# Issue order of the wide and narrow products in a split-precision decoder trunk

## The chip, the cores and the metric

The kernel runs on one core of a Trainium2 chip. The metric is the device time of one execution in microseconds (us). Three runs of the kernel before gave 2563.05, 2563.5 and 2563.72 us; the median is 2563.5 us.

## What is computed

A trunk of two pre-norm residual layers over 256 tokens of width 2048, in float32. Layer 0 mixes tokens with a Mamba-2 state-space mixer, layer 1 with a short gated convolution; each is followed by a gated feed-forward block with a convolution, and a norm closes the trunk.

```python
def reference(x, ...):
    for i in range(DEPTH):                       # DEPTH = 2
        h = rms_norm(x, mix_norm_w[i])
        if i % 2 == 0:
            x = x + ssd_mixer(h, ...)            # h @ (2048 x 10304), conv, scan, gate, @ (4096 x 2048)
        else:
            x = x + short_conv_mixer(h, ...)     # h @ (2048 x 6144), conv, gate, @ (2048 x 2048)
        h = rms_norm(x, ffn_norm_w[i])
        x = x + conv_ffn(h, ...)                 # h @ (2048 x 11264), conv, silu(g) * v, @ (5632 x 2048)
    return rms_norm(x, final_norm_w)
```

Nearly all of the arithmetic is the matrix products with the weights, some 115 M weights in all, each used once for 256 tokens.

## The kernel before

A weight matrix is streamed in units of 256 rows by 512 columns (`KU = 2` blocks of 128 rows, `COLS = 512`): one DMA brings a unit into `raw`, ScalarE rounds it to the matmul type (`wh`, L287), VectorE subtracts to get the rest (`wl`, L288). `wh` and `wl` have four buffers each (`WB = 4`), so a new unit is written when the unit four before it has been used up. The activations are held in the same two parts, side by side in one tile: `hl` has 256 columns of high part and then 256 of low part.

`stream` multiplies one block of 512 weight columns with all the rows. Its output is four column blocks `t` of 128, on the partitions of two PSUM tiles: `pts[0]` holds column blocks 0 and 1, `pts[1]` blocks 2 and 3; there are three such tiles in PSUM. For each unit it goes over `t` and, inside, over the two row blocks `k`; a (`t`, `k`) is one wide product (L334: `wh` against high and low part together, 512 columns) and one narrow product (L335: `wl` against the high part, 256 columns), added up in the same place of PSUM. Each has its own 128x128 stationary operand, so each comes with a weight load (PEld). With `one=True` (the streams for B, C and xs of the state-space mixer, where all must end in one 256-column sum) the wide product is made as two narrow ones (L331, L332). After the last unit `evac` reads both PSUM tiles out. There are 96 calls of `stream`; the down projection of the last layer has its own loop (L858 to L860, all products 512 wide).

The program is recorded in the order of the Python code, and a scheduler then puts the instructions of each engine in an order of its own choice, by when it reckons that operands are ready; only instructions given to `pin` keep the recorded order. The first stream of all (`before` given) is pinned. Small products of other kinds ("aux": transposes, sums over tokens, the scan of the mixer) are put in between.

Of the kernel before, what the change touches and what calls it, by code (L numbers as in the profile page):

```python
# [8 lines left out]
F32 = mybir.dt.float32  # L9
# [7 lines left out]
P = 128  # L17
T = 256
D = 2048
NKD = D // P  # L20
DI = 4096
NG = 8
# [3 lines left out]
DS = 128  # L26
# [6 lines left out]
KU = 2  # L33
COLS = 512
WB = 4
# [4 lines left out]
def trunk_kernel(ctx, tc, a, out):  # L40
    nc = tc.nc
    mm = nc.tensor.matmul
# [13 lines left out]
    psm = ctx.enter_context(tc.tile_pool(name="psm", bufs=3, space=PSUM))  # L56
    psa = ctx.enter_context(tc.tile_pool(name="psa", bufs=2, space=PSUM))

    n_id = [0]

    def uid(s):
        n_id[0] += 1
        return f"{s}_{n_id[0]}"
# [11 lines left out]
    start = ExitStack()  # L75
    tokpool = start.enter_context(tc.tile_pool(name="tokpool", bufs=1))
    xt = tokpool.tile([P, 2, D], F32, tag="xt", name="xt")
    pin = tc.keep_in_program_order
# [44 lines left out]
    base, at = {}, 0  # L123
    pieces = [[] for _ in range(nrt)]
    for name, r in rows:
        base[name] = at
        lo = 0
        while lo < r.shape[0]:
            i, off = divmod(at, P)
            n = min(P - off, r.shape[0] - lo)  # L130
# [3 lines left out]
        if name == "mix":  # L134
            n_mix, at = at, P
# [90 lines left out]
    plan = []  # L226
# [31 lines left out]
    raws, units = [], []  # L258
    taken = [0]

    def load_raw():
        i = len(raws)
        w, c0, kc = plan[i]
        raw = rawpool.tile([P, KU, COLS], F32, tag="raw", name=uid("raw"))
        for k in range(0, KU, 1 if i == 0 else KU):
            n = 1 if i == 0 else KU
            ins = nc.sync.dma_start(
                out=raw[:, k : k + n, :],
                in_=w[(kc + k) * P : (kc + k + n) * P, c0 : c0 + COLS].rearrange(
                    "(k p) n -> p k n", p=P  # L270
                ),
            )
            if i < NKD // KU + 2:
                pin(ins)
        raws.append(raw)

    def load_unit():
        i = len(units)
        if i == len(raws):
            load_raw()  # L280
        raw, raws[i] = raws[i], None
        wh = wpool.tile([P, KU, COLS], F32R, tag="wh", name=uid("wh"))
        wl = wpool.tile([P, KU, COLS], F32R, tag="wl", name=uid("wl"))
        units.append((wh, wl))

        def half(ks, put):
            put(nc.scalar.copy(wh[:, ks, :], raw[:, ks, :]))  # L287
            put(tt(  # L288
                out=wl[:, ks, :], in0=raw[:, ks, :], in1=wh[:, ks, :].bitcast(F32),
                op=ALU.subtract,  # L290
            ))

        if i == 0:
            return half
        with tc.high_priority(0 if i < NKD // KU else None):
            half(slice(0, KU), pin if i < NKD // KU + 2 else lambda ins: ins)

    def weight_unit(c0, kc, ahead=WB - 1):

        i = taken[0]  # L300
        assert plan[i][1:] == (c0, kc), (plan[i], c0, kc)
        taken[0] += 1
        while len(units) < min(i + ahead + 1, len(plan)):
            load_unit()
        got, units[i] = units[i], None
        return got

    def stream(c0, hls, kcs, evac, one=False, before=None):

        pts = [psm.tile([P, 2, 512], F32, tag="main", name=uid("main")) for _ in range(2)]
        n = len(kcs)
        put = (lambda ins: ins) if before is None else pin
        for u in range(0, n, KU):
            order = [(t, k) for t in range(4) for k in range(KU)]
            if before is not None and u == 0:
                before(0)
                order.sort(key=lambda tk: tk[1])  # L320
            wh, wl = weight_unit(c0, kcs[u], WB - 1 if before is None else 0)
            for at, (t, k) in enumerate(order):
                if before is not None and at == (0 if u else 2) and u + KU < n:
                    before(u // KU + 1)
                i = u + k
                o = pts[t // 2][:, t % 2, :]
                hl = hls[i // 2][:, i % 2, :]
                lw = slice(t * P, (t + 1) * P)
                first, last = i == 0, i == n - 1
                if one:  # L330
                    put(mm(o[:, 0:T], wh[:, k, lw], hl[:, 0:T], start=first, stop=False))  # L331
                    put(mm(o[:, 0:T], wh[:, k, lw], hl[:, T : 2 * T], start=False, stop=False))  # L332
                else:
                    put(mm(o, wh[:, k, lw], hl, start=first, stop=False))  # L334
                put(mm(o[:, 0:T], wl[:, k, lw], hl[:, 0:T], start=False, stop=last))  # L335
        if before is not None:
            before(n // KU)
        if taken[0] < len(plan):
            while len(units) < min(taken[0] + WB - 1, len(plan)):
                load_unit()  # L340
        for p in range(2):
            evac(p, pts[p])

# [7 lines left out]
    def scaled(pt, r, one=False, tag="tp", pool=None):  # L351
        if one:
            s = pair_tmp(tag, pool)
            tt(out=s, in0=pt[:, :, 0:T], in1=rep2(r), op=ALU.mult)  # L354
            return s
        s = pair_sum(pt)
        tt(out=s, in0=s, in1=rep2(r), op=ALU.mult)  # L357
        return s

    def conv(s, width, wname, nk, k0, bname=None, tag="tp", pool=None):  # L360

        y = pair_tmp(tag, pool)
        for j in range(2):
            w = pcol(wname, (width - 1) * nk + k0 + j)
            if bname is None:
                act(y[:, j, :], s[:, j, :], AF.Copy, scale=w)
            else:
                act(y[:, j, :], s[:, j, :], AF.Identity, bias=pcol(bname, k0 + j), scale=w)  # L368
            for d in range(1, width):
                stt(  # L370
                    out=y[:, j, d:T], in0=s[:, j, 0 : T - d],
                    scalar=pcol(wname, (width - 1 - d) * nk + k0 + j),
                    in1=y[:, j, d:T], op0=ALU.mult, op1=ALU.add,
                )
        return y
# [27 lines left out]
    xp, xhl = [], []  # L403
    ss = small.tile([P, 2, 4], F32, tag="ss", name="ss")
    first = {}
# [50 lines left out]
    def bc_stream(g, o, before=None):  # L456

        res = []

        def evac(p, pt):  # L460
            k0 = DI // P + o * NG + g + 2 * p
            s = scaled(pt, first["r0"], True)
            y = conv(s, W_SSD, "ssdw", NCX, k0, "ssdb", "bc", bcpool)
            act(y, y, AF.Silu)
            res.append(y)

        stream(2 * DI + o * NG * DS + g * DS, xhl, range(NKD), evac, True, before)
        return res

    load_raw()  # L470
# [293 lines left out]
    xhl, nhl = nhl, []  # L764
    r = norm.row()
    norm = Norm()
    for part in range(2):
        hid = ffn_part(0, part, xhl, r)
        last = part == 1
# [6 lines left out]
    xhl, nhl = nhl, []  # L776
# [32 lines left out]
    xhl = nhl  # L809
# [3 lines left out]
    for c in range(2):  # L813
        for q in range(4):
            ps = aux()
            for j in range(4):
                k = 4 * q + j
# [22 lines left out]
    for part in range(2):  # L840
        lo, hi = FPARTS[part]
        hid = ffn_part(1, part, xhl, r)
        n = hi - lo
        for cg in range(D // COLS):
            cols = slice(cg * COLS, (cg + 1) * COLS)
            pt = psm.tile([P, 2, 512], F32, tag="main", name=uid("main"))
            end = part == 1 and cg == D // COLS - 1
            lag = WB - 2 if end else 0
            held = {}

            def products(c, u):
                wh, wl = held[u]
                for k in range(KU):
                    i = u + k
                    hl = hid[i // 2][:, i % 2, :]
                    hi_ = hl[:, c * P : (c + 1) * P]
                    lo_ = hl[:, T + c * P : T + (c + 1) * P]
                    mm(pt[:, c, :], hi_, wh[:, k, :], start=(i == 0), stop=False)  # L858
                    mm(pt[:, c, :], hi_, wl[:, k, :], start=False, stop=False)  # L859
                    mm(pt[:, c, :], lo_, wh[:, k, :], start=False, stop=(i == n - 1))  # L860

            def evac(c):
                x = xtok[c][:, cols]
                tt(out=x, in0=pt[:, c, :], in1=x, op=ALU.add)  # L864
                if part == 1:
                    junk = tmp.tile([P, 512], F32, tag="tp", name=uid("tp"))
                    act(junk, x, AF.Square, accum_out=ss[:, c, cg : cg + 1])
                    tt(out=x, in0=x, in1=fin[:, cols], op=ALU.mult)
                if end:
                    finish(c)  # L870

            for u in range(0, n + lag * KU, KU):
                if u < n:
                    held[u] = weight_unit(cg * COLS, lo + u, 1 if end else WB - 1)
                    products(0, u)
                    if u == n - KU and end:
                        evac(0)
                if u >= lag * KU:
                    products(1, u - lag * KU)
            if not end:  # L880
                evac(0)
            evac(1)
# [30 lines left out]
```

## Time and profile before

| | us |
|---|---|
| median of three runs | 2563.5 |
| the profiled execution | 2563.32 |
| its span, first to last instruction | 2561.5 |
| TensorE matmul (PE) busy | 2544.6 |
| weight loads (PEld) busy | 2235.2 |
| VectorE (DVE) busy | 1790.2 |
| ScalarE (ACT) busy | 1321.5 |

A matmul's row lasts from its start until its result is out, and the next one starts well before that, so the mean length of a row says nothing of the rate. The rate is read from the starts: so many starts in a row, divided into the time from the first to the last. The timeline view gives starts to 0.01 us and merges neighbours of the same line into one row with a count (x2).

### The profile page before, as it was taken

The numbers are of one execution on the slowest core, as the hardware profiler recorded it, in microseconds if no ns is written. First come the engines' busy times: TensorE is split into PE (matmuls) and PEld (weight loads), VectorE is DVE, ScalarE is ACT, GpSimd is POOL, SyncE is SP. The second block draws the span as 40 slices with busy tenths as digits, with TensorE's granted clock in tenths as the row PEclk, the third lists the DMA queues.
The fourth block names the chain that finished last, engine by engine and source line by source line (L and its number), as shares of the span: only waits on it lengthen the run. The fifth ranks groups of instructions, "written<-read, shape, count | busy, mean of one in ns | idle before, by whom it ended". The sixth has DMA issues, their size and how long they took to land.

```text
span 2561.5 us, 38324 instructions
## 1 busy us (share of the span) xinstructions
PE 2544.6 (99%) x15101; PEld 2235.2 (87%) x15101; DVE 1790.2 (70%) x2601; ACT 1321.5 (52%) x1630; POOL 1.1 (0%) x8
## 2 busy tenths in 40 slices
PE   9999999999999999999999999999999999999998
PEld 9999998998888888888888888888888888888886
DVE  7888876788677776557776666666677774577765
ACT  5565643566555554345554444444555553455543
POOL 0000000000000000000000000000000000000000
PEclk9999999999999999999999999999999999999999
DMA  7666655665666665666665666666566666666664
GB/s 229 175 184 193 182 176 188 189 182 172 198 183 191 190 188 181 193 188 183 193 190 181 193 186 185 185 197 189 174 183 187 189 197 190 193 186 188 189 192 145
DMA packets 255737, 478.76 MB, mean 187 GB/s; under 512 B 17668, under 2 KB 29124, under 8 KB 255428
## 3 DMA queue, kind: packets, MB, share of 16 engines
q1 hardware_dynamic: 254643, 474.13, 61.3%
q8 instruction: 118, 1.93, 0.3%
q10 hardware_dynamic: 912, 2.18, 0.2%
q14 instruction: 64, 0.52, 0.1%
HBM read 474.09 MB, written 2.16 MB: 186 GB/s over the span
## 4 chain that ended last, share of the span: by engine, by line
PE 98%; DVE 1%; ACT 1%; DMA 0%; issue 0%; SPq 0%; DVEq 0%; ACTq 0%
PE main L334 50%; PE main L335 29%; PE main L331 3%; PE main L332 3%; PE main L858 3%; PE main L859 3%; PE main L860 3%; PE aux L649 1%; DVE wl L288 0%; PE aux L657 0%; DMA bias_bc<-in_ssd_dt_bias_dram 0%; PE aux L513 0%; PE aux L630 0%; DMA raw<-in_ssd_w_in_dram 0%; ACT wh L287 0%; PE aux L187 0%
## 5 line engine op out<-in xcount | busy, mean ns | idle before, releaser
L334 PE MATMUL main<-hl,wh 128*128 128x512 f32 x5568 | 1944.9, 396 | 0.2 <-DVE hl L218 0.2
L335 PE MATMUL main<-hl,wl 128*128 128x256 f32 x6336 | 1749.2, 281 | 1.8 <-DVE wl L288 1.8
L288 DVE TENSOR_TENSOR wl<-raw,wh 128x1024 fp32r<-128x1024 f32 (+1 forms) x881 | 1072.6, 1221 | 702.2 <-ACT wh L287 701.6
L287 ACT CAST wh<-raw 128x1024 fp32r<-128x1024 f32 (+1 forms) x881 | 920.8, 1048 | 1067.7 <-PE main L334 735.2
L334 PEld LDWEIGHTS main<-hl,wh 128*128 128x128 f32 x5568 | 1034.8, 188 | 236.7 <-issue 2.0
L335 PEld LDWEIGHTS main<-hl,wl 128*128 128x128 f32 x6336 | 1196.9, 189 | 17.6 <-DVE wl L288 2.7
L331 PE MATMUL main<-hl,wh 128*128 128x256 f32 x768 | 219.5, 287 | 2.5 <-DVE tp L354 1.3
L332 PE MATMUL main<-hl,wh 128*128 128x256 f32 x768 | 218.6, 285 | 0.0
L331 PEld LDWEIGHTS main<-hl,wh 128*128 128x128 f32 x768 | 148.2, 193 | 4.0 <-issue 2.0
L332 PEld LDWEIGHTS main<-hl,wh 128*128 128x128 f32 x768 | 148.3, 193 | 1.5 <-issue 1.1
L858 PE MATMUL main<-wh,hl 128*128 128x512 f32 x352 | 137.5, 391 | 0.8 <-DVE xtok L864 0.8
L859 PE MATMUL main<-wl,hl 128*128 128x512 f32 x352 | 137.4, 390 | 0.0
L860 PE MATMUL main<-wh,hl 128*128 128x512 f32 x352 | 137.0, 389 | 0.0
L370 DVE SCALAR_TENSOR_TENSOR tp<-tp,prm,tp 128x255 f32<-128x255 f32 x208 | 90.6, 477 | 0.0
L346 ACT COPY tp<-main 128x512 f32<-128x512 f32 x128 | 74.3, 580 | 26.0 <-PE main L335 26.0
L348 DVE TENSOR_TENSOR tp<-main,tp 128x512 f32<-128x512 f32 x128 | 87.4, 683 | 0.0
L858 PEld LDWEIGHTS main<-wh,hl 128*128 128x128 f32 x352 | 66.1, 188 | 15.3 <-DVE xtok L864 1.2
L860 PEld LDWEIGHTS main<-wh,hl 128*128 128x128 f32 x352 | 66.1, 188 | 14.2
L859 PEld LDWEIGHTS main<-wl,hl 128*128 128x128 f32 x352 | 66.1, 188 | 13.6
L370 DVE SCALAR_TENSOR_TENSOR g<-tp,prm,g 128x254 f32<-128x254 f32 (+1 forms) x176 | 74.6, 477 | 0.1
L368 ACT ACTIVATE g<-tp,prm,prm 128x256 f32<-128x256 f32 x88 | 48.2, 596 | 38.0 <-DVE tp L357 38.0
L357 DVE TENSOR_TENSOR tp<-tp,rrow 128x512 f32<-128x512 f32 x96 | 66.0, 688 | 1.8
(134 smaller groups left out, 966.9 us busy)
## 6 DMA issues: line engine op xcount, KB each, us to landing
raw<-in_ffn_w_up_dram SPq DMA_DIRECT2D x352, 512.0 KB, 3.7
raw<-in_ffn_w_down_dram SPq DMA_DIRECT2D x176, 512.0 KB, 4.1
raw<-in_ssd_w_in_dram SPq DMA_DIRECT2D x159, 512.0 KB, 4.5
raw<-in_sc_w_in_dram SPq DMA_DIRECT2D x96, 512.0 KB, 4.1
raw<-in_ssd_w_out_dram SPq DMA_DIRECT2D x64, 512.0 KB, 4.2
raw<-in_sc_w_out_dram SPq DMA_DIRECT2D x32, 512.0 KB, 4.2
cbc<-cs_d SPq DMA_DIRECT2D x32, 256.0 KB, 5.1
xt<-in_x_dram SPq DMA_DIRECT2D x8, 256.0 KB, 7.4
```

The lines of the kernel that those rows point to most:

```text
L287: put(nc.scalar.copy(wh[:, ks, :], raw[:, ks, :]))
L288: put(tt(out=wl[:, ks, :], in0=raw[:, ks, :], in1=wh[:, ks, :].bitcast(F32), op=ALU.subtract,))
L331: put(mm(o[:, 0:T], wh[:, k, lw], hl[:, 0:T], start=first, stop=False))
L332: put(mm(o[:, 0:T], wh[:, k, lw], hl[:, T : 2 * T], start=False, stop=False))
L334: put(mm(o, wh[:, k, lw], hl, start=first, stop=False))
L335: put(mm(o[:, 0:T], wl[:, k, lw], hl[:, 0:T], start=False, stop=last))
L346: nc.scalar.copy(pb, pt[:, :, T : 2 * T])
L348: tt(out=s, in0=pt[:, :, 0:T], in1=pb, op=ALU.add)
L370: stt(out=y[:, j, d:T], in0=s[:, j, 0 : T - d], scalar=pcol(wname, (width - 1 - d) * nk + k0 + j), in1=y[:, j, d:T], op0=ALU.mult, op1=ALU ...
L858: mm(pt[:, c, :], hi_, wh[:, k, :], start=(i == 0), stop=False)
L859: mm(pt[:, c, :], hi_, wl[:, k, :], start=False, stop=False)
L860: mm(pt[:, c, :], lo_, wh[:, k, :], start=False, stop=(i == n - 1))
```

## The change

Each (`t`, `k`) no longer goes wide, narrow. For each column block, `stream` now issues the wide products of both row blocks of a unit, and then both narrow ones. A new helper `follow` ties each of these products to the one before it, so that the scheduler keeps the recorded order; the loop of the last down projection is tied in the same way. The unit is worked in two halves: `pts[0]` with unit `u`, then `pts[1]` with unit `u - 1`; a unit is thus held over two steps, and `pts[1]` ends one half later. Weights are asked for two units ahead before the first half and three units ahead after the second. In the `one=True` streams the order in a column block is high, low, high, low, rest, rest. The first stream is now a function of its own, `first_stream`, with the order that it had.

```diff
+    def follow(inst):
+        if last_main[0] is not None:
+            tc.add_manual_dep(
+                inst.ins, last_main[0],
+                mybir.DependencyInfo(
+                    mybir.DependencyClass.NoSync, mybir.DependencyReason.DATA
+                ),
+                reason="stream order",
+            )
+        last_main[0] = inst.ins.name
+        return inst
...
+    def load_ahead(n):
+        while len(units) < min(taken[0] + n, len(plan)):
+            load_unit()
...
-    def stream(c0, hls, kcs, evac, one=False, before=None):
...
-        for u in range(0, n, KU):
-            order = [(t, k) for t in range(4) for k in range(KU)]
...
-                    put(mm(o, wh[:, k, lw], hl, start=first, stop=False))
-                put(mm(o[:, 0:T], wl[:, k, lw], hl[:, 0:T], start=False, stop=last))
...
+    def stream(c0, hls, kcs, evac, one=False):
+        pts = [psm.tile([P, 2, 512], F32, tag="main", name=uid("main")) for _ in range(2)]
+        n = len(kcs)
+        held = {}
+        def half(p, u):
+            wh, wl = held[u]
+            for t in (2 * p, 2 * p + 1):
+                o = pts[p][:, t % 2, :]
+                lw = slice(t * P, (t + 1) * P)
+                part = [(u + k, k, hls[(u + k) // 2][:, (u + k) % 2, :]) for k in range(KU)]
+                for i, k, hl in part:
+                    if one:
+                        for c in (0, T):
+                            follow(mm(
+                                o[:, 0:T], wh[:, k, lw], hl[:, c : c + T],
+                                start=(i == 0 and c == 0), stop=False,
+                            ))
+                    else:
+                        follow(mm(o, wh[:, k, lw], hl, start=(i == 0), stop=False))
+                for i, k, hl in part:
+                    follow(mm(
+                        o[:, 0:T], wl[:, k, lw], hl[:, 0:T], start=False, stop=(i == n - 1)
+                    ))
+        for u in range(0, n + KU, KU):
+            if u < n:
+                held[u] = weight_unit(c0, kcs[u], WB - 2)
+                half(0, u)
+            if u:
+                half(1, u - KU)
+            load_ahead(WB - 1)
         for p in range(2):
             evac(p, pts[p])
...
-                    mm(pt[:, c, :], hi_, wh[:, k, :], start=(i == 0), stop=False)
+                    follow(mm(pt[:, c, :], hi_, wh[:, k, :], start=(i == 0), stop=False))
```

PE's own order at the start of a stream of layer 0's first down projection, before: `main_10551` and `main_10552` are the PSUM tiles of the first and the second pair of column blocks, `wh`/`wl` with one number and the next are one unit's weights (10483, 10505, 10527 and 10555 are the first four units), `hl` a pair of row blocks of the activations.

```order
L334 MATMUL main_10551<-hl_8606,wh_10527 128x512
L335 MATMUL main_10551<-hl_8606,wl_10528 128x256
L334 MATMUL main_10551<-hl_8606,wh_10527 128x512
L335 MATMUL main_10551<-hl_8606,wl_10528 128x256
L334 MATMUL main_10551<-hl_8622,wh_10555 128x512
L334 MATMUL main_10552<-hl_8192,wh_10483 128x512
L335 MATMUL main_10552<-hl_8192,wl_10484 128x256
L334 MATMUL main_10552<-hl_8192,wh_10483 128x512
L335 MATMUL main_10552<-hl_8192,wl_10484 128x256
```

The same start of the stream on PE now (units 10491, 10513, 10535):

```order
L376 MATMUL main_10282<-hl_10278,wl_10470 128x256 x2
L374 MATMUL main_10551<-hl_8192,wh_10491 128x512 x2
L376 MATMUL main_10551<-hl_8192,wl_10492 128x256 x2
L374 MATMUL main_10551<-hl_8192,wh_10491 128x512 x2
L376 MATMUL main_10551<-hl_8192,wl_10492 128x256 x2
L374 MATMUL main_10551<-hl_8208,wh_10513 128x512 x2
L376 MATMUL main_10551<-hl_8208,wl_10514 128x256 x2
L374 MATMUL main_10551<-hl_8208,wh_10513 128x512 x2
L376 MATMUL main_10551<-hl_8208,wl_10514 128x256 x2
L374 MATMUL main_10552<-hl_8192,wh_10491 128x512 x2
```

Wide and narrow alternated, and the first pair of column blocks ran three units ahead of the second at a stream's start; now two wide go before two narrow, and the first pair is never more than two units ahead.

VectorE's order around the same place, before (`x_190` and `x_221` are the residual tiles that read out the two PSUM tiles of the stream that ended):

```order
L288 TENSOR_TENSOR wl_10506<-raw_10503,wh_10505 128x1024 [waits DMAHW6_49,PE_49,Activation_49]
L288 TENSOR_TENSOR wl_10528<-raw_10525,wh_10527 128x1024 [waits DMAHW7_49,PE_49,Activation_49]
L698 TENSOR_TENSOR x_190<-main_10281,x_190 128x512 [waits PE_49]
L698 TENSOR_TENSOR x_221<-main_10282,x_221 128x512 [waits PE_49]
L700 TENSOR_TENSOR x_190<-main_10281,x_190 128x512 [waits DVE_49]
L700 TENSOR_TENSOR x_221<-main_10282,x_221 128x512 [waits DVE_49]
L288 TENSOR_TENSOR wl_10556<-raw_10553,wh_10555 128x1024 [waits DMAHW0_49,Activation_49]
```

And now:

```order
L302 TENSOR_TENSOR wl_10514<-raw_10511,wh_10513 128x1024 [waits DMAHW6_49,PE_49,Activation_49]
L748 TENSOR_TENSOR x_190<-main_10281,x_190 128x512 [waits PE_49]
L750 TENSOR_TENSOR x_190<-main_10281,x_190 128x512 [waits DVE_49]
L302 TENSOR_TENSOR wl_10536<-raw_10533,wh_10535 128x1024 [waits DMAHW7_49,PE_49,Activation_49]
L748 TENSOR_TENSOR x_221<-main_10282,x_221 128x512 [waits PE_49]
L302 TENSOR_TENSOR wl_10564<-raw_10561,wh_10563 128x1024 [waits DMAHW0_49,Activation_49]
L750 TENSOR_TENSOR x_221<-main_10282,x_221 128x512 [waits DVE_49]
```

The four reads of PSUM stood together between two units; now a unit's subtraction stands between the first tile's reads and the second's.

## Rows read from the trace of the kernel before

**Rows 1.** The page: span, and busy us (share) xinstructions of each engine; clock granted per slice.
```profile
span 2561.5 us, 38324 instructions
PE 2544.6 (99%) x15101; PEld 2235.2 (87%) x15101; DVE 1790.2 (70%) x2601; ACT 1321.5 (52%) x1630; POOL 1.1 (0%) x8
...
PEclk9999999999999999999999999999999999999999
```
**Rows 2.** The page: the chain that ended last, its shares by engine and by line.
```profile
PE 98%; DVE 1%; ACT 1%; DMA 0%; issue 0%; SPq 0%; DVEq 0%; ACTq 0%
PE main L334 50%; PE main L335 29%; PE main L331 3%; PE main L332 3%; PE main L858 3%; PE main L859 3%; PE main L860 3%; PE aux L649 1%; DVE wl L288 0%; PE aux L657 0%; DMA bias_bc<-in_ssd_dt_bias_dram 0%; PE aux L513 0%; PE aux L630 0%; DMA raw<-in_ssd_w_in_dram 0%; ACT wh L287 0%; PE aux L187 0%
```
**Rows 3.** The page's groups: line, operation, count, busy us, mean ns, idle before.
```profile
L334 PE MATMUL main<-hl,wh 128*128 128x512 f32 x5568 | 1944.9, 396 | 0.2 <-DVE hl L218 0.2
L335 PE MATMUL main<-hl,wl 128*128 128x256 f32 x6336 | 1749.2, 281 | 1.8 <-DVE wl L288 1.8
L288 DVE TENSOR_TENSOR wl<-raw,wh 128x1024 fp32r<-128x1024 f32 (+1 forms) x881 | 1072.6, 1221 | 702.2 <-ACT wh L287 701.6
L287 ACT CAST wh<-raw 128x1024 fp32r<-128x1024 f32 (+1 forms) x881 | 920.8, 1048 | 1067.7 <-PE main L334 735.2
...
L331 PE MATMUL main<-hl,wh 128*128 128x256 f32 x768 | 219.5, 287 | 2.5 <-DVE tp L354 1.3
...
L858 PE MATMUL main<-wh,hl 128*128 128x512 f32 x352 | 137.5, 391 | 0.8 <-DVE xtok L864 0.8
```
**Rows 4.** Groups on PE, from 740 to 1140 us (layer 0's feed-forward block).
```profile
L334 PE MATMUL main<-hl,wh 128*128 128x512 f32 x1142 | 398.2, 396 | 0.0
```
**Rows 5.** Timeline of PE (start us, us), wide products alone, last layer's down projection.
```profile
2109.68 0.39 PE L858 MATMUL main<-wh,hl 128*128 128x512 f32 x1
...
2113.99 0.39 PE L859 MATMUL main<-wl,hl 128*128 128x512 f32 x1
```
**Rows 6.** Timeline of PE, narrow products alone, a `one=True` stream.
```profile
299.74 0.28 PE L335 MATMUL main<-hl,wl 128*128 128x256 f32 x1
...
302.50 0.28 PE L332 MATMUL main<-hl,wh 128*128 128x256 f32 x1
```
**Rows 7.** Timeline of PE, 1295 to 1303 us, feed-forward block.
```profile
1295.24 0.40 PE L334 MATMUL main<-hl,wh 128*128 128x512 f32 x1
...
1299.75 0.62 PE L334 MATMUL main<-hl,wh 128*128 128x512 f32 x2
1300.20 0.28 PE L335 MATMUL main<-hl,wl 128*128 128x256 f32 x1
1300.32 0.40 PE L334 MATMUL main<-hl,wh 128*128 128x512 f32 x1
...
1302.44 0.40 PE L334 MATMUL main<-hl,wh 128*128 128x512 f32 x1
1302.68 0.40 PE L335 MATMUL main<-hl,wl 128*128 128x256 f32 x2
1302.91 0.40 PE L334 MATMUL main<-hl,wh 128*128 128x512 f32 x1
```
**Rows 8.** Timeline of PE, 995 to 998 us, feed-forward block.
```profile
995.87 0.64 PE L334 MATMUL main<-hl,wh 128*128 128x512 f32 x2
996.35 0.28 PE L335 MATMUL main<-hl,wl 128*128 128x256 f32 x1
...
997.39 0.40 PE L335 MATMUL main<-hl,wl 128*128 128x256 f32 x2
997.63 0.40 PE L334 MATMUL main<-hl,wh 128*128 128x512 f32 x1
```
**Rows 9.** Waits: engine and line, waited for: us in total, times, longest us.
```profile
ACT wh L287 <- PE main L334: 735.2, 492, 6.1
...
PE main L335 <- DVE wl L288: 1.8, 3, 1.4
```
**Rows 10.** Busy us (x) of each engine from 100 to 250 us (state-space mixer).
```profile
100.00:250.00 150.00, 149.41 (x1084) 135.83 (x1083) 132.08 (x281) 96.26 (x116) 0.00 (x0) 1.00 0.66 191
```

More of the change, by code (lines that the diff above doesn't have):

```diff
@@ L59, in trunk_kernel @@
     n_id = [0]
+    last_main = [None]
+    def follow(inst):
[9 more added lines that the diff above has]
+        return inst
     def uid(s):
@@ L302, in weight_unit, with first_stream @@
         taken[0] += 1
-        while len(units) < min(i + ahead + 1, len(plan)):
-            load_unit()
+        load_ahead(ahead)
         got, units[i] = units[i], None
         return got
-    def stream(c0, hls, kcs, evac, one=False, before=None):
+    def first_stream(c0, hls, kcs, evac, before):
         pts = [psm.tile([P, 2, 512], F32, tag="main", name=uid("main")) for _ in range(2)]
         n = len(kcs)
-        put = (lambda ins: ins) if before is None else pin
         for u in range(0, n, KU):
@@ L317, in stream @@
             order = [(t, k) for t in range(4) for k in range(KU)]
-            if before is not None and u == 0:
+            if u == 0:
                 before(0)
                 order.sort(key=lambda tk: tk[1])
-            wh, wl = weight_unit(c0, kcs[u], WB - 1 if before is None else 0)
+            wh, wl = weight_unit(c0, kcs[u], 0)
             for at, (t, k) in enumerate(order):
-                if before is not None and at == (0 if u else 2) and u + KU < n:
+                if at == (0 if u else 2) and u + KU < n:
@@ L324, in stream @@
                     before(u // KU + 1)
                 i = u + k
-                o = pts[t // 2][:, t % 2, :]
+                o = pts[t // 2][:, t % 2, 0:T]
                 hl = hls[i // 2][:, i % 2, :]
                 lw = slice(t * P, (t + 1) * P)
[L329 to L333, printed above, removed]
-                    put(mm(o, wh[:, k, lw], hl, start=first, stop=False))
@@ L335, in stream @@
-                put(mm(o[:, 0:T], wl[:, k, lw], hl[:, 0:T], start=False, stop=last))
[L336 to L340, printed above, removed]
+                pin(mm(o, wh[:, k, lw], hl[:, 0:T], start=(i == 0), stop=False))
+                pin(mm(o, wh[:, k, lw], hl[:, T : 2 * T], start=False, stop=False))
+                follow(pin(mm(o, wl[:, k, lw], hl[:, 0:T], start=False, stop=(i == n - 1))))
@@ new lines, in first_stream @@
+        before(n // KU)
+        load_ahead(WB - 1)
+        for p in range(2):
+            evac(p, pts[p])
+    def stream(c0, hls, kcs, evac, one=False):
[27 more added lines that the diff above has]
+                half(1, u - KU)
+            load_ahead(WB - 1)
@@ L465, in evac @@
             res.append(y)
-        stream(2 * DI + o * NG * DS + g * DS, xhl, range(NKD), evac, True, before)
+        c0 = 2 * DI + o * NG * DS + g * DS
+        if before is not None:
+            first_stream(c0, xhl, range(NKD), evac, before)
+        else:
+            stream(c0, xhl, range(NKD), evac, True)
         return res
@@ L857, in products @@
                     lo_ = hl[:, T + c * P : T + (c + 1) * P]
-                    mm(pt[:, c, :], hi_, wh[:, k, :], start=(i == 0), stop=False)
-                    mm(pt[:, c, :], hi_, wl[:, k, :], start=False, stop=False)
-                    mm(pt[:, c, :], lo_, wh[:, k, :], start=False, stop=(i == n - 1))
+                    follow(mm(pt[:, c, :], hi_, wh[:, k, :], start=(i == 0), stop=False))
+                    follow(mm(pt[:, c, :], hi_, wl[:, k, :], start=False, stop=False))
+                    follow(mm(pt[:, c, :], lo_, wh[:, k, :], start=False, stop=(i == n - 1)))
             def evac(c):
```

## The prediction

> **What bounds the kernel now.** I read the page's first two parts, then the chain, then the groups, then the starts of products in the timeline. PE is busy 2544.6 of 2561.5 us at the full granted clock in every slice [rows 1], which is the level of 2.4 GHz. The chain that ended last runs over PE for 98% of the span, half of it in L334 and 29% in L335 [rows 2]; DVE and ACT have a part of 1% each. PE hardly waits for anybody: 1.8 us in all for the subtraction that makes `wl` [rows 3, 9]. So a change that does not make PE wait is worth what it changes in the rate at which PE takes one product after the other, and nothing else.
>
> That rate is read from starts. 400 us of the feed-forward block hold 1142 rows of L334 and nothing but wide and narrow products [rows 4]; 400/1142 is 350.3 ns for one wide and one narrow, and 350.6 if the one that had begun before the window is taken off. I use 350.5 ns for a pair. Products of one width alone run like this: wide, 19 starts in 4.31 us [rows 5], 226.8 ns each; narrow, 23 starts in 2.76 us [rows 6], 120.0 ns each. A wide and a narrow at these rates make 346.8 ns. So the alternation costs 3.7 ns a pair over what the two kinds take among their own.
>
> Where the 3.7 ns sit is seen in [rows 7]. From 1295.24 to 1299.75 there are 13 pairs in 4.51 us: 346.9 ns, nothing lost. Then two wide stand together (the scheduler had put them so), and from 1300.32 to 1302.44 there are 6 pairs in 2.12 us: 353.3 ns. The alternating stream thus has two rates, it keeps one for as long as the pattern is undisturbed, and a break in the pattern moves it to the other. The mean of 350.5 says that it spends a little over half of its time, (350.5 - 346.9)/(353.3 - 346.9) = 56%, at the slower one.
>
> **The change part by part.** The instructions are the same, in number and in shape: 5568 wide products, as many narrow ones among them (6336 less the 768 of the `one=True` streams) [rows 3], with the same weight loads. What changes is who stands beside whom.
>
> *The order in a column block.* The rows that come nearest to two wide, two narrow are the places where the scheduler left doubles. Two wide from their start to the next narrow one took 1300.20 - 1299.75 = 0.45 us in the fast stretch [rows 7], and 996.35 - 995.87 = 0.48 us in a slow one [rows 8]. Two narrow took 1302.91 - 1302.68 = 0.23 us [rows 7] and 997.63 - 997.39 = 0.24 us [rows 8]. So four products of the new order lie between 0.45 + 0.23 = 0.68 us and 0.48 + 0.24 = 0.72 us; four of the old one take 2 x 350.5 = 701 ns. By rows 5 and 6 they take 2 x 226.8 + 2 x 120.0 = 693.6 ns, and I take this value. The reason is in the same rows: a double of narrow ones took 0.23 to 0.24 us, its own rate or less, in both stretches, so that the wide pair behind it starts without a debt, and the wide pair that so starts is the one of 0.45 us; the 0.48 us stand only behind alternating products at the slow rate, which the new order does not have. It also halves the number of changes of width. The gain is 350.5 - 346.8 = 3.7 ns for each of 5568 pairs, 20.6 us. I do not count on all of it: streams end, small products come in between, and after each such break the order must find its rate again. I leave a tenth of the stretch at the slower rate of rows 7, 0.1 x (353.3 - 346.8) x 5568 = 3.6 us.
>
> *The `one=True` streams and the last down projection.* All products of the first have 256 columns, all of the second 512, so their order changes no neighbour's width: 120.0 and 226.8 ns before and after [rows 5, 6]. Nothing.
>
> *The second pair a unit behind.* A half unit is four pairs, 4 x 350.5 = 1.4 us. Before, a unit was read for two halves on end; now from its first use over three halves (its first, the next unit's first, its own second), so its buffer comes free 1.4 us later. There are four buffers and a unit lasts 2.8 us, so from free to needed again there were 8.4 us and are 7.0. In these the rounding on ACT (1.05 us) and the subtraction on DVE (1.22 us) must be done [rows 3], and what else stands in their queues. Queued behind a subtraction that waits on DVE are the reads of PSUM and the convolutions of the stream that ended, and behind those in turn the next units; on ACT the copies out of PSUM stand behind the rounding. At a stream's start the new order is the gentler one: before, the first pair of column blocks took three units and began a fourth in 4.2 us, now it takes two and then alternates with the second pair. The cover is seen in the waits: the rounding waited 492 times for PE to set a buffer free, up to 6.1 us, and PE 3 times for a subtraction [rows 9]. Losing 1.4 us of such a lead costs nothing where DVE has time. The least it has is in the mixer, 132 of 150 us busy [rows 10]; there I allow 0 to 3 us, and take 0.
>
> *The tie between products.* It adds no wait across engines. What the scheduler could pull forward when an operand was late it cannot now; it was late 3 times for 1.8 us [rows 9]. I bound this at 0 to 2 us and take 0. The DMA queue on SP sees the same loads in the same order.
>
> **The sum.** Against the profiled execution, 2563.3 us (its span and 1.8 us around it; the median of the three runs is 0.2 us higher): 2563.3 - 20.6 + 3.6 = 2546.3 us, 0.7% faster. I predict 2546 us.
>
> **The rivals.** A measurement of this kernel can tell 0.2% from no change, 5.1 us: below 2558.2 is faster, above 2568.4 slower.
>
> *A tax for each change of width.* The loss of 3.7 ns may hang on going from wide to narrow and back, wherever it happens, and be paid once for every four products now: half of it stays. 2563.3 - 10.3 = 2553 us. For it speaks that the streams of one width lose nothing [rows 5, 6]; against it that half the alternating stretches lose nothing either [rows 7].
>
> *The order does not matter.* The two doubles of wide products average 0.465 us and the two of narrow ones 0.235 us, 0.70 us together, which is two pairs as they are now [rows 4, 7, 8]. Then the new order also has two rates, spends as much time at each as the old one, and the time stays at 2563 us, within 2 us. [...]
>
> *A slower rate of its own.* The new order may lock, as the old one does, but at the doubles of rows 8: 0.48 + 0.24 = 0.72 us for four products, 19 ns over now, and since it is fixed nothing would ever move it off. That is 2784 x 19 ns = 53 us, 2616 us, if it held everywhere; it decides where the mean four reaches 701 + 1.8 ns (5.1 us over 2784 fours), that is where (702.8 - 693.6)/(720 - 693.6), a third of the fours, are of that kind. For it: such doubles exist. Against it: the narrow double after it in rows 8 was followed by the fast rate.
>
> *PE waits for weights.* The 1.4 us less of lead may be lacking at the ends of streams, where DVE and ACT also read PSUM out. It decides from (20.6 + 5.1)/96 = 0.27 us in each of the 96 streams; a subtraction's length, 1.22 us, in each would be 117 us less the gain, 2660 us. Against it stand rows 9 and the gentler start.
>
> **How the numbers follow.** The forecast, 2540 to 2549 us: 0.52. A tax for each change, 2549 to 2558: 0.16. The order does not matter, 2558 to 2568: 0.15. A slower rate of its own: 0.10, most of it mild, 2568 to 2600. Waits for weights: 0.07, of which half would still leave it within 0.2% or faster. So faster by over 0.2% has 0.69, within 0.2% 0.17, slower 0.14. The range that holds 8 in 10 goes from 2539 (the whole gain, and 3 us more of gaps at breaks) to 2568 us; what is left out is mostly the slower end.
>
> **What would show it.** Right, if in the profile after the timeline of a feed-forward block has four products, from the first wide one to the next first wide one, in 0.69 to 0.70 us over tens of such fours, with two wide in 0.45 us, and if 400 us hold some 1151 wide rows and not 1142. The tax would show as 0.697 us, the third case as 0.70 with long stretches at either rate, the fourth as 0.71 or more. Waits for weights would show as PE waiting for L302 for tens of us, and DVE's wait for PE, not PE's rate, would be what moved. Wrong also, if the fours run at 0.693 us and the time does not follow: then breaks at stream ends took it back.

## The result, and the profile after

The changed kernel takes 2575.1 us (2572.4 to 2575.9 in five runs) against 2563.1 us before: a ratio of 1.0044 with a 95% interval of 1.0029 to 1.0059. It is slower, by 0.3 to 0.6%; the forecast was 0.7% faster, and the range ended at 2568.

The page of after, span and busy time [rows 1]:

```profile
span 2573.3 us, 38332 instructions
...
PE 2540.4 (99%) x15101; PEld 2231.6 (87%) x15101; DVE 1796.3 (70%) x2601; ACT 1328.0 (52%) x1630; POOL 1.1 (0%) x8
```

The same products, 11.8 us more span and 4.2 us less busy time on PE: PE stood still 32.9 us (2573.3 - 2540.4) and not 16.9. Where, is read from a line that both programs have: VectorE scales a sum read out of PSUM by the norm's row. Its first two rows are the read-outs of the first and the second pair of column blocks of the first feed-forward stream, right behind the mixer; its last row is near the end of the last such stream. This is the view of the line (its count, ns of one, first and last start), and then its second row in the timeline, of before:

```profile
L357 DVE TENSOR_TENSOR tp<-tp,rrow x96: 679/691/695, 735.9 to 2446.4; 128x512 f32<-128x512 f32 x96
739.38 0.68 DVE L357 TENSOR_TENSOR tp<-tp,rrow 128x512 f32<-128x512 f32 x1
```

And of after:

```profile
L403 DVE TENSOR_TENSOR tp<-tp,rrow x96: 679/691/695, 754.5 to 2458.4; 128x512 f32<-128x512 f32 x96
760.03 0.69 DVE L403 TENSOR_TENSOR tp<-tp,rrow 128x512 f32<-128x512 f32 x1
```

The second row is the mark from here on. The first would flatter the change: with the lag, the first pair of column blocks ends earlier in its stream, and its read-out stands 5.5 us ahead of the second pair's, not 3.4. Up to the mark, after lost 760.0 - 739.4 = 20.6 us. From the mark to the last row it won: 1698.4 us and not 1707.0, 8.6 us. Behind the last they agree to 0.2 us. So there are two results: a gain behind the mixer, where PE runs undisturbed, and a loss in the mixer more than twice as large.

**The gain.** Groups on PE of after, 800 to 1200 us, 400 us with nothing but wide and narrow products [rows 4]:

```profile
L374 PE MATMUL main<-hl,wh 128*128 128x512 f32 x1150 | 360.9, 395 | 0.0
```

The timeline of PE, after [rows 7]:

```profile
1294.96 0.63 PE L374 MATMUL main<-hl,wh 128*128 128x512 f32 x2
1295.42 0.40 PE L376 MATMUL main<-hl,wl 128*128 128x256 f32 x2
...
1302.62 0.63 PE L374 MATMUL main<-hl,wh 128*128 128x512 f32 x2
```

1150 wide rows stand in place of 1142. From 1294.96 to 1302.62 there are 11 fours in 7.66 us, 696.4 ns each: one steady rate, no second one, between the 693.6 ns of the forecast and the 701 ns of before.

**The loss.** What PE waited for in the whole execution (engine, line, what it waited for: us, times, longest), after [rows 9]:

```profile
PE main L376 <- DVE wl L302: 5.3, 5, 2.3
PE aux L680 <- ACT xs L625: 5.1, 5, 1.0
PE aux L201 <- DVE dg L193: 3.1, 1, 3.1
PE aux L163 <- DVE prm L164: 2.1, 2, 1.9
PE main L374 <- DVE hl L232: 1.8, 1, 1.8
```

All of it lies in the first 660 us, and less than a third is the wait for weights that I had listed. Most of the rest are small products whose operand is late and which stand in PE's order ahead of other products. The timeline of PE near the end of the mixer shows the longest. L208 sums over tokens for the norm of the scan's last group, L201 spreads the result, and the stream of the down projection that is running needs it for its last units:

```profile
648.66 0.50 PE L208 MATMUL aux<-ones,nacc 128*128 128x1 f32 x4
...
650.40 0.40 PE L376 MATMUL main<-hl,wl 128*128 128x256 f32 x2
653.88 1.09 PE L201 MATMUL aux<-dg,ones 128*128 128x128 f32 x4 [3.08 <-DVE dg L193]
656.81 1.22 PE L374 MATMUL main<-hl,wh 128*128 128x512 f32 x2 [1.84 <-DVE hl L232]
657.83 0.63 PE L376 MATMUL main<-hl,wl 128*128 128x256 f32 x2
```

And the same place before (the sum is L194, the spread L187):

```profile
634.57 0.50 PE L194 MATMUL aux<-ones,nacc 128*128 128x1 f32 x4
...
639.88 0.38 PE L187 MATMUL aux<-dg,ones 128*128 128x128 f32 x2
```

From sum to spread it is 5.2 us after and 5.3 us before: VectorE's chain is as long as it was. Before, 28 products stood between the two in PE's order and filled the time; now 9 do, and PE stands still for 3.1 us, then 1.8 us more for the activations (`hl`) made from the result. Which part of the change does this is seen in the experiments. There is a second price in these rows: the wide pair behind the wait takes 657.83 - 656.81 = 1.02 us and not 0.46. Busy us (x) of each engine (the first number is PE's), then the granted clock, DMA share and GB/s, of after:

```profile
20.00:60.00 40.00, 35.71 (x277) 35.08 (x275) 29.70 (x62) 22.11 (x32) 0.00 (x0) 0.91 0.61 182
40.00:50.00 10.00, 6.85 (x33) 6.63 (x34) 8.84 (x19) 5.44 (x9) 0.00 (x0) 0.66 0.54 186
...
100.00:130.00 30.00, 26.17 (x146) 20.83 (x146) 26.34 (x54) 16.23 (x20) 0.00 (x0) 0.94 0.64 194
130.00:600.00 470.00, 464.60 (x3300) 423.61 (x3297) 372.21 (x691) 266.72 (x316) 0.00 (x0) 1.00 0.62 182
...
640.00:670.00 30.00, 25.08 (x133) 21.56 (x132) 20.23 (x39) 13.07 (x21) 0.00 (x0) 0.89 0.56 174
```

After each of the three longest stretches of waiting (around 42, 115 and 652 us), the granted clock falls for a few us from its full level, 2.4 GHz, to the lower one, 1.2 GHz: to 0.91, 0.94 and 0.89 in the mean of the three stretches shown around them. Before, it is 1.00 in every ten us up to 700 us. So a wait is paid for a second time in part: beside the 16.0 us more for which PE stands still, the lower clock takes at most 0.09 x 40 + 0.06 x 30 + 0.11 x 30 = 8.7 us of work in these stretches.

### The profile page after: what moved, and what is told of

Same layout as the page of the kernel before. It is cut to its first block, busy times and chain, and to the rows that moved or that the text cites. A ratio compares the mean times of both kernels' runs of the same rounds, so it can differ in the third digit from the quotient of the medians.

```text
span 2573.3 us, 38332 instructions
## 1 busy us (share of the span) xinstructions
PE 2540.4 (99%) x15101; PEld 2231.6 (87%) x15101; DVE 1796.3 (70%) x2601; ACT 1328.0 (52%) x1630; POOL 1.1 (0%) x8
## 4 chain that ended last, share of the span: by engine, by line
PE 75%; DVE 0%; ACT 0%; issue 0%; ACTq 0%
PE main L374 44%; PE main L376 22%; PE main L908 3%; PE main L909 3%; PE main L910 3%; PE aux L868 0%; PE aux L201 0%; PE aux L699 0%; DVE xtok L914 0%; PE aux L208 0%; ACT xtok L883 0%; DVE yg L735 0%; DVE wl L302 0%; ACT wh L301 0%; PE aux L707 0%; DVE xtok L885 0%
## 5 line engine op out<-in xcount | busy, mean ns | idle before, releaser
L374 PE MATMUL main<-hl,wh 128*128 128x512 f32 x5568 | 1753.7, 396 | 2.6 <-DVE hl L232 1.8
L302 DVE TENSOR_TENSOR wl<-raw,wh 128x1024 fp32r<-128x1024 f32 (+1 forms) x881 | 1074.8, 1222 | 703.6 <-ACT wh L301 699.1
L376 PEld LDWEIGHTS main<-hl,wl 128*128 128x128 f32 x6272 | 1156.6, 189 | 254.2 <-DVE wl L302 7.0
L376 PE MATMUL main<-hl,wl 128*128 128x256 f32 x6272 | 1244.4, 280 | 5.3 <-DVE wl L302 5.3
L374 PEld LDWEIGHTS main<-hl,wh 128*128 128x128 f32 x5568 | 849.8, 189 | 4.2 <-DVE hl L232 2.1
L369 PE MATMUL main<-hl,wh 128*128 128x256 f32 x1408 | 231.6, 286 | 1.3 <-DVE tp L400 1.3
L369 PEld LDWEIGHTS main<-hl,wh 128*128 128x128 f32 x1408 | 197.0, 194 | 2.5 <-issue 2.5
L908 PEld LDWEIGHTS main<-wh,hl 128*128 128x128 f32 x352 | 66.1, 188 | 15.3 <-DVE xtok L914 1.2
L909 PEld LDWEIGHTS main<-wl,hl 128*128 128x128 f32 x352 | 66.1, 188 | 13.5
L414 ACT ACTIVATE tp<-tp,prm,prm 128x256 f32<-128x256 f32 x88 | 48.0, 593 | 0.0
L416 DVE SCALAR_TENSOR_TENSOR xs<-tp,prm,xs 128x253 f32<-128x253 f32 (+2 forms) x96 | 40.7, 473 | 0.0
```

What stands on the lines that cost most here:

```text
L302: put(tt(out=wl[:, ks, :], in0=raw[:, ks, :], in1=wh[:, ks, :].bitcast(F32), op=ALU.subtract,))
L369: follow(mm(o[:, 0:T], wh[:, k, lw], hl[:, c : c + T], start=(i == 0 and c == 0), stop=False,))
L374: follow(mm(o, wh[:, k, lw], hl, start=(i == 0), stop=False))
L376: follow(mm(o[:, 0:T], wl[:, k, lw], hl[:, 0:T], start=False, stop=(i == n - 1)))
L416: stt(out=y[:, j, d:T], in0=s[:, j, 0 : T - d], scalar=pcol(wname, (width - 1 - d) * nk + k0 + j), in1=y[:, j, d:T], op0=ALU.mult, op1=ALU ...
L908: follow(mm(pt[:, c, :], hi_, wh[:, k, :], start=(i == 0), stop=False))
```

## The experiments

The diff makes three changes at once: the order of widths, the tie between products, the lag of the second pair of column blocks. Seven kernels separate them. The marks of all of them (second and last row of the line above, in each kernel's profile), with the median time:

| kernel | order | tie | lag | mark, us | mark to last, us | median, us |
|---|---|---|---|---|---|---|
| before | alternating | no | no | 739.4 | 1707.0 | 2563 |
| after | two, two | yes | yes | 760.0 | 1698.4 | 2575.1 |
| e1_no_tie | two, two | no | yes | 742.8 | 1699.1 | 2559.1 |
| e2_no_lag | two, two | yes | no | 751.1 | 1702.5 | 2570.7 |
| e3_alternate | alternating | yes | yes | 760.9 | 1708.7 | 2590.9 |
| e7_tie_alone | alternating | yes | no | 752.7 | 1708.9 | 2580.0 |
| e4_ffn_only | mixer as before, then as after | | | 739.5 | 1698.4 | 2555.9 |
| e6_mixer_free | as e4, two, two in the mixer too | | | 735.8 | 1698.4 | 2551.6 |
| e5_four_four | as e4, four, four behind the mixer | | | 739.4 | 1706.5 | 2564.9 |

**Without the tie.**

```diff
-        if last_main[0] is not None:
+        if False:
             tc.add_manual_dep(
```

> The changed kernel without the tie between products: recorded in the same order with the same lag, but the scheduler may move products again (it leaves 2531 of the doubles of wide ones). If the tie is what makes PE wait in the mixer (it may no longer pass a product or a small product whose operand is late), the 21 us that are lost up to 670 us go back to under 5, and the time is 2553 to 2558 us. If the lag of the second pair of column blocks is the cause, the loss stays at 15 us or more and the time is 2570 to 2576 us. Both theories expect the rate of the feed-forward blocks to stay near that of the changed kernel, 22.3 to 22.4 us for a stream of 8 units.

Measured: 2559.1 us, ratio 0.9982 (0.9973 to 0.9991). The mark is 17.2 us earlier than in after. The rate stays (1699.1 us), though the scheduler moved products and left 2531 doubles of wide ones. The tie carries most of the loss. The time is just above the range that I gave (2553 to 2558): 742.8 us is still 7.0 us more than the mixer needs without the lag (e6_mixer_free). Busy time and clock of e1_no_tie, to be laid beside those of after, and two of its waits:

```profile
20.00:60.00 40.00, 37.58 (x314) 37.21 (x313) 32.95 (x67) 25.30 (x35) 0.00 (x0) 1.00 0.64 200
...
100.00:130.00 30.00, 30.00 (x210) 26.63 (x209) 25.82 (x58) 18.27 (x21) 0.00 (x0) 1.00 0.64 198
130.00:600.00 470.00, 470.00 (x3320) 429.75 (x3319) 378.32 (x708) 263.58 (x316) 0.00 (x0) 1.00 0.63 187
...
630.00:670.00 40.00, 34.92 (x189) 29.49 (x189) 26.27 (x47) 15.93 (x22) 0.00 (x0) 0.91 0.52 166
```

```profile
PE aux L201 <- DVE dg L193: 2.8, 1, 2.8
...
PE main L374 <- DVE hl L232: 1.8, 1, 1.8
```

So the tie's price lies ahead of the place whose timeline is shown above. In the first three of these stretches PE stands still 13.5 us in after and 2.4 us here, and after loses up to 5.4 us more to the lower clock. At the scan's last norm both stand still some 5 us and both have the lower clock behind it: the wait from sum to spread is there without the tie too, with no product at all between the two.

**Without the lag.**

```diff
-        for u in range(0, n + KU, KU):
-            if u < n:
-                held[u] = weight_unit(c0, kcs[u], WB - 2)
-                half(0, u)
-            if u:
-                half(1, u - KU)
-            load_ahead(WB - 1)
+        for u in range(0, n, KU):
+            held[u] = weight_unit(c0, kcs[u], WB - 1)
+            half(0, u)
+            half(1, u)
+        load_ahead(WB - 1)
```

> The changed kernel with both pairs of column blocks on the same unit, tie and order wide, wide, narrow, narrow kept, weights asked for three units ahead as before. If the lag is the cause of the loss in the mixer, the loss up to 670 us falls from 21 to under 6 us and the time is 2553 to 2559 us. If the tie is the cause, the loss stays at 15 us or more and the time is 2570 to 2578 us. Without the lag the fixed order has no slack where the read-out of PSUM must set the second pair free at a stream's start: a wait there would show as PE waiting for the read-out in the feed-forward blocks, up to 1 us for each of the 84 streams with wide products; I expect less than 0.1 us each.

Measured: 2570.7 us, ratio 1.0026 (1.0017 to 1.0035). The mark moves back by 8.9 us, the tie's part of the loss stays. The five waits for `xs` are gone; near the end of the mixer PE waits 0.3 us for the spread and 2.8 us for `hl`. What PE waits for, e2_no_lag:

```profile
PE aux L163 <- DVE prm L164: 2.9, 1, 2.9
PE main L374 <- DVE hl L232: 2.8, 1, 2.8
PE aux L645 <- DVE prm L164: 2.3, 1, 2.3
```

In PE's order the second four transposes of `xs` stand 74 products of the streams behind the end of the xs stream in the five groups of after that wait, 1.0 us each, for ScalarE. In the same groups they stand 80 or 82 behind it here, and 73 or 79 before, and none waits. So the distance alone does not decide it; why these wait is open. In the feed-forward blocks the view of waits shows none for the read-out of PSUM without the lag, but the stretch behind the mark took 1702.5 us, 4.1 more than with it: nearly half of the gain hangs on the lag. In the timeline of PE the fours break once in each of twelve streams behind the mark; two fours then take 0.93 and 0.78 us and not 0.70 each, 3.7 us in all, without a wait that the profile names. After has no such break. One of them, e2_no_lag:

```profile
1026.80 0.62 PE L374 MATMUL main<-hl,wh 128*128 128x512 f32 x2
1027.26 0.39 PE L376 MATMUL main<-hl,wl 128*128 128x256 f32 x2
1027.73 0.71 PE L374 MATMUL main<-hl,wh 128*128 128x512 f32 x2
1028.28 0.41 PE L376 MATMUL main<-hl,wl 128*128 128x256 f32 x2
1028.52 0.63 PE L374 MATMUL main<-hl,wh 128*128 128x512 f32 x2
```

**Alternating again, tie and lag kept.**

```diff
                 for i, k, hl in part:
                     ...
-                for i, k, hl in part:
                     follow(mm(
                         o[:, 0:T], wl[:, k, lw], hl[:, 0:T], start=False, stop=(i == n - 1)
                     ))
```

> The changed kernel with wide and narrow products in turn again, tie and lag kept. Both theories on the mixer expect its loss to stay, 18 to 22 us up to 670 us. It measures what the order of widths alone is worth: if the loss per change of width is real, the streams of the feed-forward blocks take 22.4 us or more for 8 units and the time is 8 to 13 us above the changed kernel, 2582 to 2588 us. If the gain in rate came from the undisturbed order and not from the doubles, the time stays at 2572 to 2577 us.

Measured: 2590.9 us, ratio 1.0107 (1.0091 to 1.0124). The mixer's loss stays (760.9 us); the stretch behind the mark takes 1708.7 us, 10.3 more than in after. So the gain in rate is the order of widths, and not that an order was fixed: the alternating order when tied is even a little slower than before (1707.0). The median is 3 us over my range and 4.7 us over the profiled execution (2584.4 us of span and 1.8 around it), so the size of this one is the least certain. Its profile also shows that the lower clock does not follow every such wait. From 40 to 50 us PE stands still 2.7 us (3.2 in after), at full clock:

```profile
40.00:50.00 10.00, 7.29 (x58) 6.97 (x58) 8.95 (x19) 5.34 (x10) 0.00 (x0) 1.00 0.54 185
```

**The change behind the mixer only.** The streams of the mixer go through a copy of the old function, without `follow`.

```diff
+    new_order = [False]
...
     def stream(c0, hls, kcs, evac, one=False):
+        (new_stream if new_order[0] else old_stream)(c0, hls, kcs, evac, one)
...
     mixer.close()
+    new_order[0] = True
```

> The mixer of layer 0 as in the kernel before (order, no lag, no tie), and the changed streams from the first feed-forward block on. If all the loss sits in the mixer and all the gain behind it, as the comparison of the two traces says (21 us lost up to 669 us, 8.9 us won after), the time is 2552 to 2556 us, 7 to 11 us below the kernel before. If the later part owes its gain to something that the mixer's part sets up (the phase of the buffers, say), the time is 2560 us or more.

Measured: 2555.9 us, ratio 0.9968 (0.9956 to 0.9979), as expected. The mark is at 739.5 us, as before, and the stretch behind it takes 1698.4 us, as in after. The loss is the mixer's and the gain is the rest's; the change is not bad as such but in the wrong place.

**Four wide, four narrow**, on e4_ffn_only.

```diff
-            for t in (2 * p, 2 * p + 1):
-                ...
+            part = [
+                (pts[p][:, t % 2, :], slice(t * P, (t + 1) * P), u + k, k,
+                 hls[(u + k) // 2][:, (u + k) % 2, :])
+                for t in (2 * p, 2 * p + 1) for k in range(KU)
+            ]
+            for o, lw, i, k, hl in part:
+                follow(mm(o, wh[:, k, lw], hl, start=(i == 0), stop=False))
+            for o, lw, i, k, hl in part:
+                follow(mm(
+                    o[:, 0:T], wl[:, k, lw], hl[:, 0:T], start=False, stop=(i == n - 1)
+                ))
```

> The kernel e4_ffn_only with four wide and then four narrow products (both column blocks of a pair) in the tied streams from the first feed-forward block on. If a loss is paid for each change from wide to narrow and back, 3.3 ns for a group however long it is (two, two: 696.6 ns against 693.3 by the rates of one width), half of what is left goes: a stream of 8 units takes 22.24 us and not 22.29, 68 such streams in lengths of 8 to 12 units give some 4 us, and the time is 2551 to 2553 us. If two, two has its own rate for another reason, the groups of four may lie anywhere from 22.19 (no loss at all) to 22.4 us a stream, 2547 to 2563 us.

Measured: 2564.9 us, ratio 1.0004 (0.9994 to 1.0013): all of the gain is gone, and the time is 2 us above the widest range that I gave. The timeline of PE, e5_four_four:

```profile
1300.38 1.09 PE L396 MATMUL main<-hl,wh 128*128 128x512 f32 x4
1301.31 0.64 PE L398 MATMUL main<-hl,wl 128*128 128x256 f32 x4
...
1304.59 1.09 PE L396 MATMUL main<-hl,wh 128*128 128x512 f32 x4
```

Three eights in 4.21 us are 1403 ns each, 16 ns over the 1387.2 ns that the rates of one width make; two fours of after take 1392.8, 6 ns over. Half as many changes of width cost nearly three times as much. So the loss is not a price for each change of width, and the agreement of 696 ns with the first rival of the prediction is a coincidence. What sets the rate of a pattern is open.

**Two, two in the mixer, without tie and lag**, on e4_ffn_only: the body of `old_stream` records, for each `t`, the wide products of both `k` and then the narrow ones.

```diff
-                for k in range(KU):
-                    ...
-                        mm(o, wh[:, k, lw], hl, start=first, stop=False)
-                    mm(o[:, 0:T], wl[:, k, lw], hl[:, 0:T], start=False, stop=last)
+                for i, k, hl in part:
+                    ...
+                        mm(o, wh[:, k, lw], hl, start=(i == 0), stop=False)
+                for i, k, hl in part:
+                    mm(o[:, 0:T], wl[:, k, lw], hl[:, 0:T], start=False, stop=(i == n - 1))
```

> The kernel e4_ffn_only with wide, wide, narrow, narrow recorded in the mixer too, there without tie and without lag. If the order of widths alone costs nothing and only tie and lag cost in the mixer, its 16 streams with wide products gain 0.1 us each and the time is 2553 to 2556 us, a little under e4_ffn_only. If the order itself makes PE wait in the mixer (the rest of a unit's products asked for in another place), the time is 2560 us or more.

Measured: 2551.6 us, ratio 0.995 (0.9935 to 0.9965). It is the fastest of all, 0.5% below the kernel before, and 1.4 us better than I expected at best. The mark, e6_mixer_free:

```profile
735.80 0.69 DVE L430 TENSOR_TENSOR tp<-tp,rrow 128x512 f32<-128x512 f32 x1
```

The order of widths wins 3.7 us in the mixer too (735.8 against 739.5). In this kernel the transposes, the sum and the spread are again placed by the scheduler with whatever products it finds.

**The tie alone.** The kernel before with every product of a stream tied to the one before it.

```diff
-        put = (lambda ins: ins) if before is None else pin
+        put = follow if before is None else pin
```

> The kernel before with the tie alone: wide and narrow in turn, no lag. If the tie makes PE wait in the mixer by itself, the mixer up to unit 200 takes 9 to 15 us more than in the kernel before (646 to 652 us) as in e2_no_lag, and the time is 2570 to 2580 us. If tie and lag are only harmful together (e2_no_lag lost something through its order of widths), the time is 2560 to 2566 us. The transposes of xs stand 82 or more products behind the end of the xs stream here, against 60 to 64 in the changed kernel, so their waits of 1.4 us a group should be gone by any theory.

Measured: 2580.0 us, ratio 1.0065 (1.0048 to 1.0081), at the upper end of the range for a tie that costs by itself. The mark, e7_tie_alone:

```profile
752.65 0.68 DVE L371 TENSOR_TENSOR tp<-tp,rrow 128x512 f32<-128x512 f32 x1
```

The mark is 13.3 us late from the tie alone, and the waits for `xs` are absent, as expected. What PE waits for:

```profile
PE aux L163 <- DVE prm L164: 3.8, 2, 2.9
PE main L348 <- DVE tp L368: 3.7, 2, 3.1
PE main L348 <- DVE hl L232: 2.8, 1, 2.8
```

The transposes of the parameters (L163) wait only in the kernels that are tied in the mixer (2.1 us in after, 2.9, 1.6 and 3.8 in e2, e3 and e7); without the tie it is 0.2 us in e6_mixer_free and none in the others. Busy time and clock from 40 to 50 us, where the first of them stand:

```profile
40.00:50.00 10.00, 6.72 (x30) 6.44 (x31) 8.10 (x18) 4.94 (x8) 0.00 (x0) 0.51 0.56 198
```

In the same ten us the kernel before is busy 8.7 us at full clock.

Taken together, the mark goes 739.4 (before), 735.8 with the order of widths (e6_mixer_free), 742.8 with the lag as well (e1_no_tie), 760.0 with the tie as well (after): -3.6, +7.0, +17.2 us, +20.6 in all. The other paths give the same order of size: the lag costs 8.9 us (e2_no_lag to after) and 8.2 us (e7_tie_alone to e3_alternate), the tie 15.3 us (e6_mixer_free to e2_no_lag) and 13.3 us (before to e7_tie_alone). In time they roughly add up, in place they do not. The waits for `xs` (5.1 us in after) come only where tie and lag are together, and those for weights are longest there (5.3 us in after, 6.0 in e3_alternate, 1.1 to 2.9 in the others); near the end of the mixer either one alone brings a wait.

## Why the prediction was wrong

*That PE bounds the kernel and only its rate counts* held for the kernel before, and is why the gain shows undiminished in e4_ffn_only and e6_mixer_free.

*The order of widths* was the right mechanism with the wrong size. I took 693.6 ns for a four and got 696.4; 3.7 ns a pair became some 2.3, and the 17.0 us that I counted on became 12.4 in the span of e6_mixer_free (2549.1 against 2561.5), part of it with the help of the lag (e2_no_lag). The rows of single doubles [rows 7, 8] could not settle it: their starts are to 10 ns, and a pattern repeated without end has a rate that no single break shows. I had weighed the half of the gain as the first rival, at 0.16, and its size came; its reason did not (e5_four_four).

*The tie* is the step that failed. I bounded it at 0 to 2 us and took 0, because PE had waited for a subtraction 3 times for 1.8 us [rows 9]. That row was the wrong one. It shows what is left after the scheduler has placed the small products and the products of the streams around each other; what the tie takes away is this freedom, and a profile in which PE is busy throughout does not show what that is worth. It measured 17.2 us beside the lag (e1_no_tie against after) and 13.3 us alone (e7_tie_alone): PE standing still for small products and for operands of its next product, and the lower clock behind that. It was not the wait from sum to spread, which the lag brings.

*The lag* I had put at 0 to 3 us in the mixer and taken 0; it measured 7.0 us without the tie and 8.2 and 8.9 us with it. I looked at the buffers of the weights. Without the tie these cost nothing (PE waited 1.5 us for L302 in e1_no_tie, 1.8 before), with it 5.3 us. But I did not follow the results of the streams to the small products that need them. From sum to spread at the scan's last norm, 9, 0 and 8 products stand in the three kernels that have the lag in the mixer (after, e1, e3), and PE waits 3.1, 2.8 and 3.2 us; in the others it is 23 to 28 products and at most 0.4 us.

*The rival of waits* had the right sign and the wrong place. I looked for it at the ends of all 96 streams; it came at some dozen places of the mixer, where products of another kind stand between. *A slower rate of its own* did not come: the fours run at one rate, a little faster than before.

*What I had no term for* is the clock. In after, the three longest stretches of waiting were each followed by products at half rate, at most 8.7 us beside 16.0 us of more standing still. In the kernel before no such stretch exists, so its profile could not show that; and the page of after has a 9 in every slice of the clock, as in [rows 1], so there it is seen only in shorter windows. It is no fixed surcharge: e3_alternate stood still nearly as long from 40 to 50 us and kept the full clock. What decides it is open here.

## What to carry to other kernels

Before a scheduler's freedom is taken away, ask what it has been hiding: find the chains on other engines (here 5 us from a sum to its spread) and count what stands on the bound engine while they run, for a change of order like the lag can empty that place too; a small wait in the profile is not the price of fixing the order but what was left of it. Fix an order only where nothing else has to be put in between, as in the feed-forward blocks here, and change one thing at a time: the order of widths, with the lag behind the mixer, was worth 0.5%, and the tie and the lag that came with it cost 0.9% in the mixer (24.2 of 2563 us).

## What the runs showed of the hardware

Wide and narrow products at full clock have rates that depend on how they are grouped, and not in step with the number of changes of width: for four of each, by the starts, 1387 ns as streams of one width [rows 5, 6], 1388 or 1413 alternating [rows 7], 1393 in groups of two, 1403 in groups of four. In these stretches PE waits for nothing and runs at full clock. Why a pattern has the rate that it has is open; no run here takes it apart further.
